# Moving the activation rows of the output projection and the feed-forward part by 80 bytes

## The chip, the cores and the metric

The kernel runs on one core of a Trainium2 chip. The metric is the device time of one execution in microseconds (us). TensorE (PE in the profile) multiplies, and its weight loads have a row of their own (PEld). VectorE (DVE) and ScalarE (ACT) do elementwise work, GpSimd (POOL) clears memory, SyncE (SP) issues the transfers. On-chip memory (SBUF) has 128 partitions; an address below is the byte offset within a partition, the same in all 128.

## The reference

One layer of a hybrid decoder works on 304 rows: 16 meta tokens, 256 prompt rows, and 8 samples of 4 rows. The parts that matter here are the dense projections; between the first two of them stand two token mixers (a recurrent one and a retention), which are left out.

```python
xn = f(rms_norm(x, norm_mix))
z = xn @ f(w_in)                                    # 2048 -> 7456
...
h = x + (jnp.concatenate([o_a, o_b], axis=-1) @ f(w_out)).astype(x.dtype)   # 2048 -> 2048
hn = rms_norm(h, norm_ffn)
h = h + (jax.nn.silu(hn @ w_gate) * (hn @ w_up)) @ w_down                   # 2048 -> 5632 -> 2048
```

The meta rows are dropped at the end, so the output projection and the feed-forward part need 288 rows only.

## The kernel before

**Layout.** Activations lie transposed: features in the partitions, tokens along the row. A matmul holds a block of 128 x 128 weights still and streams a row of 288 to 304 token columns past it into PSUM.

**Precision.** Weights and activations are split into two float32r parts, high and low. Each step of a product is three matmuls (lines 719 to 721): high weights by the high activations, high weights by the low ones, low weights by the high ones.

**Weights.** All projection weights come as one stream in the order of use (`sequence`, `steps`), 512 columns at a time: one transfer into `wr`, a cast on ACT into `wh` (`cast`), a subtraction on DVE into `wl` (`rest`), each in a ring of five buffers. `main` walks the steps, issues the three matmuls, and hands a finished accumulator to the job's `post`.

**Activations.** `xh` and `xl` hold 16 rows of XW = 320 columns each (1280 bytes). Three stages use them in turn. The input projection fills them in `convert` and streams columns c0 to 304 of every row; c0 is 0 for most tiles, 14 for the tiles called r of the recurrent mixer and for two small ones, and META = 16 for the tiles of the retention's q (line 1453, g = 0) and of its gate (line 1614), which so have 288 columns. The output projection's `prep` (lines 1711 to 1713) writes the mixers' results into columns 0 to 288, eight rows for each half. Then `hn` (line 748) writes the scaled residual into the same columns for the gate and up matmuls of the feed-forward part. The down matmuls stream `act` tiles, which `gu_post` (line 1736) makes: a high and a low row of 320 columns each, of which columns 0 to 288 are used. They come from a float32r arena with places that are planned ahead. `self.xs` is the list of row views that jobs are given.

**Order.** The feed-forward part goes through 5632 hidden features in 11 groups of four tiles of 128: the gate and up tiles of a group (16 steps each), then 16 down tiles (four steps each), with the first gate and up tiles of the next group put ahead of them. A planner (`Plan`) runs the whole program once with estimated times, writes down the order of work and the tiles' lifetimes, and the second run repeats that order. Its estimates go by shape and kind of an instruction, not by a column's position.

**Addresses.** In the built program, `xh` starts at 16512, `xl` at 36992 and the float32r arena at 215168. All are 128 past a multiple of 256, and 1280 is a multiple of 256, so each row of `xh`, `xl` and `act` starts 128 past a multiple of 256. The buffers of `wh` and `wl` start at 76608 and 86848 and follow each other by 2048; a block of 128 weight columns is 512 bytes, so every block that a matmul loads starts 64 past a multiple of 256.

Of the kernel before, what the change touches and what calls it, by code (L numbers as in the profile page):

```python
# [9 lines left out]
F32R = mybir.dt.float32r  # L10
I32 = mybir.dt.int32
AF = mybir.ActivationFunctionType
ALU = mybir.AluOpType
AX = mybir.AxisListType

P = 128
D = 2048
KT = D // P
# [4 lines left out]
T = META + SEQ + NB * NS  # L23
XW = T + 16
TO = SEQ + NB * NS
# [9 lines left out]
FSTEP = 4  # L35
# [33 lines left out]
for _n, _w in [("id", 128), ("blk", 128), ("mar", 256), ("lvl", 2 * 64), ("m16", 64), ("i16", 16), ("h16", 32), ("h32", 128), ("rst", TP),  # L69
               ("bm128", 8), ("ks", 12), ("kss", 4), ("qs", 128), ("own", 256), ("sel", 32)]:  # L70
    CV[_n] = _o
    _o += _w
NCV = _o


LASTK = T - P
# [67 lines left out]
def constants():  # L144

    f = np.float32
    c = np.zeros((P, NCV), f)
    put = lambda n, a: c.__setitem__((slice(0, a.shape[0]), slice(CV[n], CV[n] + a.shape[1])), a)
# [435 lines left out]
class Step:  # L584
# [163 lines left out]
    def hn(self, m):  # L748

        hm, gm = self.ht[m // 4][:, m % 4, :], self.pv("gffn", m)  # L750
        self.act.activation(self.xh[:, m, :TO], hm, AF.Copy, scale=gm)
        self.dve.scalar_tensor_tensor(self.xl[:, m, :TO], hm, gm, self.xh[:, m, :TO], op0=ALU.mult, op1=ALU.subtract)

    def rsqrt(self, src, scale, eps, floor=None, out=None):

# [81 lines left out]
    def constants(self):  # L837
# [5 lines left out]
        self.sp.dma_start(self.shin, I["shift"])  # L843
        self.cst = self.t([P, NCV], "cst", pool=self.cp)
        self.sp.dma_start(self.cst, I["cst"])
# [825 lines left out]
    def out_jobs(self, half):  # L1671

        dve, act = self.dve, self.act

        def post(m):
            def f(acc):
                if half == 0 and m % 4 == 0 and m < 12:
                    residual(m + 4)
                if half and m == 0:
                    self.ssq2 = self.t([P, TO], "ssq2")  # L1680
                hm = self.ht[m // 4][:, m % 4, :]
                dve.tensor_add(hm, hm, acc[:, :TO])
                if not half:
                    return
                yield
                if m < 8:
                    self.hn(m)
                if m == KT - 1:
                    for i in range(8, KT):
                        self.hn(i)  # L1690
                    self.done.add("hs")
                yield from self.sumsq(self.ssq2, hm, m == 0)
                if m == KT - 1:
                    yield
                    rstd = yield from self.rstd_from(self.ssq2)
                    self.rstd2 = self.t([P, TO], "rstd")
                    act.copy(self.rstd2, rstd)
                    self.done.add("rstd2")
            return f

        ks = range(8 * half, 8 * half + 8)

        def residual(m):
            ht = self.t([P, 4, TO], "ht")
            self.sp.dma_start(ht, xT(self.I)[:, m:m + 4, META:])
            self.ht.append(ht)

        def prep():
            if half == 0:
                residual(0)  # L1710
            for k in ks:
                act.copy(self.xh[:, k, :TO], self.os[k])
                dve.tensor_sub(self.xl[:, k, :TO], self.os[k], self.xh[:, k, :TO])

        need = lambda: all(("o", k) in self.done for k in ks)
        return [Job(("out", half, m), self.xs[8 * half:], post(m), cols=(0, TO),
                    need=None if m else need, prep=None if m else prep) for m in range(KT)]

    def ffn_jobs(self):
        dve, act = self.dve, self.act  # L1720
        hold = {}

        def gu_post(f, f0, up, acts, last):
            def g(acc):
                t = self.t([P, TO], "fu" if up else "fg")
                dve.tensor_mul(t, acc[:, :TO], self.rstd2)
                yield
                if not up:
                    act.activation(t, t, AF.Silu)
                    hold[f] = t  # L1730
                    return
                while f not in hold:
                    yield
                dve.tensor_mul(t, t, hold.pop(f))
                yield
                hl = self.t([P, 2, XW], "act", F32R)[:, :, :TO]
                act.copy(hl[:, 0, :], t)
                yield
                dve.tensor_sub(hl[:, 1, :], t, hl[:, 0, :])
                acts[f - f0] = hl[:, 0, :], hl[:, 1, :]  # L1740
                if last:
                    self.done.add(("act", f))
            return g

        def down_post(m, fin):
            def g(acc):
                hm = self.ht[m // 4][:, m % 4, :]
                if fin and m == KT - 1:

                    sq = self.t([P, TO], "sq2")  # L1750
                    third = [slice(c * TO // 3, (c + 1) * TO // 3) for c in range(3)]
                    for c in third:
                        dve.tensor_add(hm[:, c], hm[:, c], acc[:, c])
                    for c in third:
                        act.activation(sq[:, c], hm[:, c], AF.Square)
                    self.bridge()
                    yield
                    yield from self.final(sq)
                    return
                dve.tensor_add(hm, hm, acc[:, :TO])  # L1760
                if fin:
                    if m == 0:
                        self.ssq3 = self.t([P, TO], "ssq3")

                        root = self.t([P, 1], "root")
                        act.activation(root, self.ones[:, :1], AF.Sqrt)
                    yield
                    yield from self.sumsq(self.ssq3, hm, m == 0)
                    yield
                    act.activation(hm, hm, AF.Copy, scale=self.pv("gfin", m))  # L1770
            return g

        jobs = []
        for f0 in range(0, FT, FSTEP):
            f1 = min(f0 + FSTEP, FT)
            acts = {}
            for f in range(f0, f1):
                for up, name in enumerate(("gate", "up")):
                    jobs.append(Job((name, f), self.xs, gu_post(f, f0, up, acts, f == f1 - 1), cols=(0, TO),
                                    need=lambda: "hs" in self.done, ready="rstd2"))  # L1780
            for m in range(KT):
                jobs.append(Job(("down", f0, m), acts, down_post(m, f1 == FT), cols=(0, TO),
                                need=lambda f=f1 - 1: ("act", f) in self.done))
        return jobs
# [10 lines left out]
    def build(self, gam4):  # L1795
        self.gam4 = gam4
        self.shifts = 0
        self.os, self.on, self.gates, self.ht, self.xs_of = [None] * KT, {}, {}, [], {}
        self.xh = self.t([P, KT, XW], "xh", F32R, pool=self.cp)[:, :, :T]
        self.xl = self.t([P, KT, XW], "xl", F32R, pool=self.cp)[:, :, :T]  # L1800
        self.xs = [(self.xh[:, k, :], self.xl[:, k, :]) for k in range(KT)]
        jobs = [self.z_job(i, self.lora_post(i), c0=META - 2 if i else 0) for i in range(3)]
        for h in range(NPAIR):
            jobs += self.pair_jobs(h)
        for h in range(RH):
            jobs += self.ret_jobs(h) + self.gate_jobs(h)
        jobs += self.out_jobs(0) + self.out_jobs(1) + self.ffn_jobs()
        jobs = {j.key: j for j in jobs}
        self.raws, self.halves, self.rests, self.loaded, self.halved = [], [], [], 0, 0
        self.start()  # L1810
        self.plan.run(self.main(jobs))
        self.flush(all=True)
# [5 lines left out]
def xT(I):  # L1818

    return I["xT"][:, KT:].rearrange("p (k t) -> p k t", t=T)  # L1820
# [52 lines left out]
```

## Time and profile before

| | us |
|---|---|
| median of 3 runs | 1545.74 |
| lowest and highest | 1544.01, 1547.75 |
| span of the profiled execution | 1544.2 |
| PE busy | 1527.5 |
| weight loads busy | 1499.9 |
| DVE busy | 1089.4 |
| ACT busy | 866.5 |

The span is the time from the first to the last instruction of the one execution that was profiled; the device time of a run has some start and end around it. The input projection and the mixers fill the span up to some 594 us, the output projection goes on to some 695 us, the feed-forward part to 1533 us, and the last norm and the transfers out end it. A matmul's record lasts from its start to the end of its pipeline, about 294 ns here, while the next one starts some 130 ns later. The pace of TensorE is thus the distance between starts, and not the length of a record.

### The profile page before, as it was taken

How to read it: one execution, taken by the hardware profiler on the slowest of the kernel's cores; microseconds unless marked ns; L12 is line 12 of the kernel's file. 1: busy time of each engine (PE TensorE's matmuls, PEld its weight loads, DVE VectorE, ACT ScalarE, POOL GpSimd, SP SyncE). 2: the span in 40 equal slices, each digit the busy share in tenths (PEclk: the TensorE clock that was granted, in tenths of full speed). 3: DMA queues.
4: the chain of work that ended last, by engine and by line, in shares of the span. 5: the costliest groups of instructions: out<-in, count | busy, mean ns of one | idle time of the engine just before them, and what ended most of it. 6: DMA issues, size and time to landing. Idle time of an engine off the chain costs nothing.

```text
span 1544.2 us, 31919 instructions
## 1 busy us (share of the span) xinstructions
PE 1527.5 (99%) x11446; PEld 1499.9 (97%) x11446; DVE 1089.4 (71%) x2782; ACT 866.5 (56%) x2031; POOL 27.7 (2%) x161
## 2 busy tenths in 40 slices
PE   9999999999999999999999999999999999999997
PEld 8999999999999998999999999999999999999997
DVE  6989789899989878676656555556565656565656
ACT  6775876787876865555444444444444444444446
POOL 1000000000000000000000000000000000000000
PEclk9999999999999999999999999999999999999998
DMA  7544445434444576655555555555555555555553
GB/s 229 175 144 141 124 113 153 126 115 155 157 124 136 182 247 210 207 171 162 167 171 164 164 168 166 169 167 169 170 162 171 164 167 168 170 165 172 162 173 117
DMA packets 136334, 252.33 MB, mean 163 GB/s; under 512 B 15984, under 2 KB 22256, under 8 KB 136176
## 3 DMA queue, kind: packets, MB, share of 16 engines
q1 hardware_dynamic: 136176, 250.29, 53.5%
q8 instruction: 91, 1.49, 0.4%
q14 instruction: 67, 0.55, 0.1%
HBM read 235.95 MB, written 14.28 MB: 162 GB/s over the span
## 4 chain that ended last, share of the span: by engine, by line
PE 88%; DVE 7%; ACT 3%; issue 1%; DMA 0%; SPq 0%; DVEq 0%; ACTq 0%
PE acc L310 78%; PE mm L310 10%; DVE arena_dt.float L310 5%; ACT arena_dt.float L310 2%; DVE wl L310 2%; ACT wh L310 1%; DMA arena_dt.float<-xT 0%; SPq L310 0%; DVE arena_dt.float32r L310 0%; ACT arena_dt.float32r L310 0%; DVE xl L310 0%; ACT xh L310 0%; DVEq L1869 0%; ACT shout L310 0%; DVEq L310 0%
## 5 line engine op out<-in xcount | busy, mean ns | idle before, releaser
L310 PE MATMUL acc<-xh,wh 128*128 128x288 f32 (+2 forms) x2592 | 789.8, 305 | 2.6 <-ACT wh L310 1.8
L310 PE MATMUL acc<-xh,wl 128*128 128x288 f32 (+2 forms) x2592 | 765.5, 295 | 0.3 <-DVE wl L310 0.3
L310 PE MATMUL acc<-xl,wh 128*128 128x288 f32 (+2 forms) x2592 | 765.1, 295 | 0.1
L310 ACT CAST wh<-wr 128x512 fp32r<-128x512 f32 (+1 forms) x827 | 501.4, 616 | 350.8 <-PE acc L310 313.0
L310 DVE TENSOR_TENSOR wl<-wr,wh 128x512 fp32r<-128x512 f32 (+1 forms) x827 | 560.2, 685 | 131.0 <-ACT wh L310 128.1
L310 PEld LDWEIGHTS acc<-xh,wh 128*128 128x128 f32 x2592 | 486.2, 188 | 9.6 <-issue 3.7
L310 PEld LDWEIGHTS acc<-xl,wh 128*128 128x128 f32 x2592 | 486.0, 188 | 4.6 <-issue 1.2
L310 PEld LDWEIGHTS acc<-xh,wl 128*128 128x128 f32 x2592 | 485.3, 187 | 1.1 <-DVE wl L310 0.6
L310 PE MATMUL acc<-arena_dt.float32r,wh 128*128 128x288 f32 x1408 | 278.9, 294 | 0.4 <-ACT arena_dt.float32r L310 0.3
L310 PEld LDWEIGHTS acc<-arena_dt.float32r,wh 128*128 128x128 f32 x1408 | 224.9, 188 | 0.9 <-ACT arena_dt.float32r L310 0.6
L310 PE MATMUL acc<-arena_dt.float32r,wl 128*128 128x288 f32 x704 | 206.7, 294 | 0.0
L310 DVE TENSOR_TENSOR arena_dt.float<-acc,arena_dt.float 128x288 f32<-128x288 f32 (+4 forms) x181 | 72.7, 420 | 167.9 <-PE acc L310 167.6
L310 DVE TENSOR_TENSOR arena_dt.float<-arena_dt.float 128x288 f32<-128x288 f32 (+22 forms) x694 | 175.2, 286 | 12.0 <-ACT arena_dt.float L310 7.6
L310 ACT ACTIVATE arena_dt.float<-arena_dt.float 128x288 f32<-128x288 f32 (+7 forms) x245 | 104.6, 433 | 116.7 <-DVE arena_dt.float L310 114.8
L310 PE MATMUL mm<-arena_dt.float 128*128 128x128 f32 (+7 forms) x1136 | 167.7, 302 | 0.6 <-issue 0.2
L310 DVE TENSOR_TENSOR arena_dt.float<-arena_dt.float,acc 128x288 f32<-128x288 f32 (+1 forms) x210 | 94.4, 451 | 95.8 <-PE acc L310 95.6
L310 PEld LDWEIGHTS mm<-arena_dt.float 128*128 128x128 f32 (+1 forms) x1136 | 141.3, 181 | 11.4 <-issue 3.6
L310 PEld LDWEIGHTS acc<-arena_dt.float32r,wl 128*128 128x128 f32 x704 | 132.1, 188 | 0.0
L310 ACT COPY arena_dt.float<-mm 64x64 f32<-64x64 f32 (+11 forms) x330 | 91.4, 286 | 49.0 <-PE mm L310 44.0
L310 ACT CAST arena_dt.float32r<-arena_dt.float 128x288 fp32r<-128x288 f32 (+4 forms) x73 | 30.5, 422 | 91.1 <-DVE arena_dt.float L310 90.4
L310 ACT COPY arena_dt.float<-arena_dt.float 128x32 f32<-128x32 f32 (+7 forms) x235 | 57.1, 293 | 13.3 <-DVE arena_dt.float L310 11.5
L310 DVE SCALAR_TENSOR_TENSOR arena_dt.float<-arena_dt.float 128x288 f32<-128x288 f32 (+3 forms) x96 | 43.1, 451 | 2.3 <-ACT arena_dt.float L310 0.5
(66 smaller groups left out, 564.8 us busy)
## 6 DMA issues: line engine op xcount, KB each, us to landing
wr<-big SPq DMA_DIRECT2D x823, 256.0 KB, 2.8
arena_dt.float<-s0r SPq DMA_DIRECT2D x16, 512.0 KB, 5.2
out_rts<-arena_dt.float SPq DMA_DIRECT2D x16, 512.0 KB, 4.4
arena_dt.float<-xT SPq DMA_DIRECT2D x4, 576.0 KB, 4.7
arena_dt.float<-lora SPq DMA_DIRECT2D x16, 128.0 KB, 2.6
arena_dt.float<-s0w SPq DMA_DIRECT2D x8, 256.0 KB, 2.9
out_rws<-arena_dt.float SPq DMA_DIRECT2D x8, 256.0 KB, 3.5
out_y<-arena_dt.float SPq DMA_DIRECT2D x7, 288.0 KB, 2.4
```

Source lines behind the costliest of these rows:

```text
L310: return self._plan.keep(f(*a, **k))
```

## The change

Two lists give, for each of the 16 rows of `xh` and `xl` and for each of the 11 groups of `act` tiles, the column at which the 288 columns begin. All entries are 20 columns, 80 bytes, and 20 + 288 still fits into the 320. `self.xf` is the list of shifted row views. `prep`, `hn`, the output jobs and the gate and up jobs use it in place of the views that began at column 0; the act tiles are cut the same way. The input projection keeps its views and columns, and neither tile sizes nor weights are touched.

```diff
+SHIFT_X = [20] * KT
+SHIFT_A = [20] * 11
...
     def hn(self, m):
 
         hm, gm = self.ht[m // 4][:, m % 4, :], self.pv("gffn", m)
-        self.act.activation(self.xh[:, m, :TO], hm, AF.Copy, scale=gm)
-        self.dve.scalar_tensor_tensor(self.xl[:, m, :TO], hm, gm, self.xh[:, m, :TO], op0=ALU.mult, op1=ALU.subtract)
+        xh, xl = self.xf[m]
+        self.act.activation(xh, hm, AF.Copy, scale=gm)
+        self.dve.scalar_tensor_tensor(xl, hm, gm, xh, op0=ALU.mult, op1=ALU.subtract)
...
             for k in ks:
-                act.copy(self.xh[:, k, :TO], self.os[k])
-                dve.tensor_sub(self.xl[:, k, :TO], self.os[k], self.xh[:, k, :TO])
+                xh, xl = self.xf[k]
+                act.copy(xh, self.os[k])
+                dve.tensor_sub(xl, self.os[k], xh)
...
-        return [Job(("out", half, m), self.xs[8 * half:], post(m), cols=(0, TO),
+        return [Job(("out", half, m), self.xf[8 * half:], post(m), cols=(0, TO),
...
-                hl = self.t([P, 2, XW], "act", F32R)[:, :, :TO]
+                s = SHIFT_A[f0 // FSTEP]
+                hl = self.t([P, 2, XW], "act", F32R)[:, :, s:s + TO]
...
-                    jobs.append(Job((name, f), self.xs, gu_post(f, f0, up, acts, f == f1 - 1), cols=(0, TO),
+                    jobs.append(Job((name, f), self.xf, gu_post(f, f0, up, acts, f == f1 - 1), cols=(0, TO),
...
-        self.xh = self.t([P, KT, XW], "xh", F32R, pool=self.cp)[:, :, :T]
-        self.xl = self.t([P, KT, XW], "xl", F32R, pool=self.cp)[:, :, :T]
+        xh = self.t([P, KT, XW], "xh", F32R, pool=self.cp)
+        xl = self.t([P, KT, XW], "xl", F32R, pool=self.cp)
+        self.xh, self.xl = xh[:, :, :T], xl[:, :, :T]
+        self.xf = [(xh[:, k, s:s + TO], xl[:, k, s:s + TO]) for k, s in enumerate(SHIFT_X)]
         self.xs = [(self.xh[:, k, :], self.xl[:, k, :]) for k in range(KT)]
```

## The prediction, made before the changed kernel was run

> **What bounds the kernel now.** I read the page first: its busy times, then the chain that ended last.
>
> ```profile
> span 1544.2 us, 31919 instructions
> ## 1 busy us (share of the span) xinstructions
> PE 1527.5 (99%) x11446; PEld 1499.9 (97%) x11446; DVE 1089.4 (71%) x2782; ACT 866.5 (56%) x2031; POOL 27.7 (2%) x161
> ...
> PE 88%; DVE 7%; ACT 3%; issue 1%; DMA 0%; SPq 0%; DVEq 0%; ACTq 0%
> ```
>
> TensorE (PE) is the bound, but a busy share of 99% does not tell how fast it goes. That is read from the chain in order of time, from 590 us on (start, length, what, count), and from the busy times of one steady stretch.
>
> ```profile
> 611.50 90.06 PE acc L310 x684
> ...
> 705.91 799.13 PE acc L310 x6069
> ...
> 800.00:1400.00 600.00, 600.00 (x4559) 600.00 (x4558) 353.94 (x634) 253.82 (x443) 0.00 (x0) 1.00 0.56 167
> ```
>
> From 611 to 1505 us nothing but PE stands on the chain, and its pace is 799.13 us / 6069 = 131.67 ns per matmul (90.06 / 684 gives the same). In the steady stretch the granted clock is 1.00, DVE is busy 59%, ACT 42%, the DMA engines 56%: each waits for PE. So the output projection and the feed-forward part cost the number of their matmuls times the interval between two starts, and nothing else in that stretch can move the end.
>
> **What the change touches.** Moved are the rows that the matmuls of these two parts stream. Their number comes from the groups by shape (count | busy us, mean ns; a mean is the length of one matmul in a pipeline, not the interval).
>
> ```profile
> L310 PE MATMUL acc<-xh,wh 128*128 128x288 f32 x1920 | 572.1, 298 | 0.8 <-ACT xh L310 0.8
> L310 PE MATMUL acc<-xl,wh 128*128 128x288 f32 x1920 | 563.9, 294 | 0.1
> L310 PE MATMUL acc<-xh,wl 128*128 128x288 f32 x1920 | 563.6, 294 | 0.0
> L310 PE MATMUL acc<-arena_dt.float32r,wh 128*128 128x288 f32 x1408 | 278.9, 294 | 0.4 <-ACT arena_dt.float32r L310 0.3
> L310 PE MATMUL acc<-arena_dt.float32r,wl 128*128 128x288 f32 x704 | 206.7, 294 | 0.0
> ```
>
> Of each 1920, 256 belong to 16 tiles of the input projection that also have 288 columns (line 1453 with g = 0, line 1614), and they stay. So 3 x 1664 + 1408 + 704 = 7104 matmuls change their start address. **One ns of interval is worth 7.1 us, or 0.46%.** No instruction, DMA or wait is added or removed.
>
> **Does the start address matter?** The kernel holds its own comparison. Those 16 tiles have the same shape and precision, and weights that lie the same, but stream from column 16 on, 64 bytes later. In the built program the rows of xh, xl and act begin on multiples of 128 bytes and every block of weights 64 bytes past one. I call the lead the distance by which the moving row's start is ahead of the weight block's, modulo 128: it is 64 now, 0 in those tiles, 120 in the tiles of 290 columns that start at column 14 (56 bytes), and 16 after the change (80 - 64). The chain has a run of the first kind and one of the 304-column tiles (lead 64); the matmuls in order of time give the 290-column tiles (first and last of 48).
>
> ```profile
> 227.26 5.60 PE acc L310 x42
> ...
> 127.58 7.03 PE acc L310 x51
> ```
>
> ```profile
> 96.30 0.30 PE L310 MATMUL acc<-xh,wh 128*128 128x290 f32 x1
> ...
> 102.57 0.30 PE L310 MATMUL acc<-xh,wl 128*128 128x290 f32 x1
> ```
>
> Lead 0: 5.60 / 42 = 133.3 ns, 1.65 ns more than 131.67 at lead 64 for the same 288 columns. Lead 120: 6.27 / 47 = 133.4 ns; from 131.67 and from the 304 columns' 7.03 / 51 = 137.8, 290 columns at lead 64 would take 131.67 + 2 x 6.13 / 16 = 132.4. So leads 0 and 120 are dearer than 64 by 1.0 to 1.65 ns. Lead 16 is in no row.
>
> The Trainium skill says otherwise (SBUF — State Buffer, Who interferes with whom): TensorE has one read port for the moving operand and another for weight loads, and waits on no one. By that rule the sum is zero. The 133.3 against 131.67 does not agree with it, unless something else in the input stage slows those tiles.
>
> **What could cost the 1.65 ns, and what lead 16 does to it.** The weight load of the next matmul runs beside the current one. The load's length gives its speed, and 32-column tiles show what a short load leaves (start of the kernel, two clocks: the windows' last three columns are granted clock, DMA share, GB/s).
>
> ```profile
> L310 PEld LDWEIGHTS acc<-arena_dt.float32r,wh 128*128 128x128 f32 x1408 | 224.9, 188 | 0.9 <-ACT arena_dt.float32r L310 0.6 <-DVE arena_dt.float32r L310 0.3
> ...
> L310 PEld LDWEIGHTS mm<-arena_dt.float 128*32 128x32 f32 x128 | 3.3, 109 | 2.7 <-issue 1.3
> ```
>
> ```profile
> 13.14 0.44 PE L310 MATMUL acc<-xh,wh 128*32 128x290 f32 x1
> ...
> 15.07 0.44 PE L310 MATMUL acc<-xh,wl 128*32 128x290 f32 x1
> ...
> 18.89 0.29 PE L310 MATMUL acc<-xh,wh 128*32 128x290 f32 x1
> ...
> 20.06 0.30 PE L310 MATMUL acc<-xh,wh 128*32 128x290 f32 x1
> ```
>
> ```profile
> 12.90:15.10 2.20, 2.20 (x10) 1.57 (x11) 2.20 (x5) 2.20 (x6) 0.00 (x0) 0.50 1.04 405
> 18.80:20.20 1.40, 1.40 (x13) 1.15 (x13) 1.40 (x4) 1.40 (x3) 0.00 (x0) 1.00 0.83 210
> ```
>
> 96 more columns take 188 - 109 = 79 ns, so 128 take 105 ns, at 4.9 bytes per ns. The moving row goes 1152 / 131.67 = 8.75 bytes per ns. While a load lasts, the moving reader gains (8.75 - 4.9) x 105 = some 400 bytes on it. If the two disturb each other each time the gain passes a multiple of 128 bytes, the places are: lead 0 at 0, 128, 256, 384 (four); lead 120 at 8, 136, 264, 392 (four); lead 64 at 64, 192, 320, and 448 just beyond the reach; lead 16 at 112, 240, 368, and 496 far beyond. This is my account, not something a row states; it fits the order of the three leads. At lead 64 the fourth lies near the edge, and two rows show that the pace there is not one fixed number: in the last group, with the same leads, it differs (first and last matmul shown, 45 intervals apart).
>
> ```profile
> 1518.08 0.43 PE L310 MATMUL acc<-arena_dt.float32r,wh 128*128 128x288 f32 x2
> ...
> 1524.03 0.43 PE L310 MATMUL acc<-arena_dt.float32r,wh 128*128 128x288 f32 x2
> ```
>
> 5.95 us / 45 = 132.2 ns against 131.67. So I take it that lead 64 meets the fourth disturbance in some matmuls and not in others, and lead 16 never.
>
> The price of "never" is not in the trace. **Bounds:** from below, the 32-column tiles at full clock, 1.17 us / 9 = 130.0 ns for 290 columns, 129.1 for 288, which is what a load a quarter as long leaves: a gain of 2.55 ns, 18 us. (At half clock they take 1.93 us / 8 = 241 ns, so 120 at full speed; no row at full clock comes near it, and I do not reach for it.) From above, lead 0, the nearest row in bytes: 1.65 ns, 11.7 us lost. I take an even mixture of three and four at lead 64, so three alone is as far below 131.67 as four is above: 130.0 ns. The sum is 7104 x -1.65 ns = **-11.7 us**; the span goes from 1544.2 to 1532.5, and the median of the runs, 1.5 us above the span, from 1545.74 to **1534.0**.
>
> The Trainium skill's interval for one matmul (TensorE: Matmul & The Clock Gate, Back-to-back issue gap) is N / 2.4 + 2.5 ns; an estimate from that page is 122.5 ns for 288 columns, and the sum by it would be 65 us saved at most. No row here at full clock shows it.
>
> **What else the shift moves.** The rows are also written 80 bytes later: 32 rows of xh and of xl (8 of them before this answer's window, which starts at 590 us), and 44 act tiles.
>
> ```profile
> L310 ACT ACTIVATE xh<-arena_dt.float,pv x16: 519/536/538, 648.0 to 696.1; 128x288 fp32r<-128x288 f32 x16
> L310 DVE SCALAR_TENSOR_TENSOR xl<-arena_dt.float,pv,xh x16: 512/516/520, 648.5 to 698.3; 128x288 fp32r<-128x288 f32 x16
> L310 ACT CAST xh<-arena_dt.float x8: 427/430/431, 641.6 to 643.9; 128x288 fp32r<-128x288 f32 x8
> L310 DVE TENSOR_TENSOR xl<-arena_dt.float,xh x8: 449/450/452, 642.7 to 645.3; 128x288 fp32r<-128x288 f32 x8
> ```
>
> I cost this at nothing: if every write took half as long again, each engine would lose 32 x 0.25 = 8 us, most of it between 640 and 700 us, and 44 x 0.22 = 10 us over the feed-forward part, under 100% in both (59% and 42% busy above). Uncovered are only the last writes before the first gate tile and before the last group of down tiles, under 2 us in all. The planner books by shape, not by column, so the order of instructions stays. If PE gets faster by 1.3%, its feeders have room: 59% becomes 60%.
>
> **The rivals.**
> Slower: the disturbance repeats every 256 bytes, not 128. Then the leads are 64 (now), 128 and 120 (dear), and 144 after the change, beyond the dear ones. With a reach of 400 bytes, lead 64 passes at 192 and sometimes 448, leads 128 and 144 at 128, 384 and at 112, 368: two each. Lead 16 then takes 133.3 ns: +11.7 us, 1557.4. It decides from the point where the second passing falls inside the reach. For it speaks that the nearest row, 16 bytes away, is dear, and that 120 to 128 rises; against it, nothing but the fit of the other account.
> Same: lead 64 meets exactly three disturbances, as lead 16 does, and the 132.2 ns is an accident of the last group; or the input stage, not the address, makes its tiles slow. The short load (one passing at 8 bytes of gain, 129.1 ns) speaks for it: one at 129.1 and four at 133.3 make 1.4 ns each, so three come to 131.9, about what lead 64 has. Then 1545.7; the skill's rule of separate ports ends here too.
> That the change does not do what it says: only if readers and writers were shifted by different amounts, and both go through the same list of views (xf), so I give it nothing.
>
> **How the numbers follow.** This kernel's measurement tells about 0.2% (3 us) from no change, 0.44 ns per matmul. Faster, 1527 to 1542: 0.44. Same: 0.20. Slower, 1549 to 1560: 0.36. The range for all is 1526 to 1560: its low end is the 129.1 ns bound with 1.5 us for the spread of the runs, its high end the lead-0 price with 2 us for late writes.
>
> **What would show it.** In the changed profile the long piece of the chain from about 705 us should again have some 6069 matmuls, at 130.0 ns each (789 us instead of 799); 133.3 (809 us) proves the slower rival, 131.7 the same. The input stage's 133.3 and 137.8 ns must stay, and the output projection's run from 611 us must change by the same ns as the feed-forward part, since all three kinds of rows get the same lead. I am wrong altogether if the interval falls below 129 or rises above 134 ns, or if PE shows gaps there.

## The result, and the profile after

| | before | changed |
|---|---|---|
| median of 4 runs on the same chip, us | 1545.9 | 1535.11 |
| lowest and highest, us | 1544.01, 1547.75 | 1533.65, 1535.58 |
| span of the profiled execution, us | 1544.2 | 1533.1 |

The ratio of the times is 0.9932, with a 95% interval from 0.9918 to 0.9946: 10.8 us faster. The forecast was 1534.0.

The page of the changed kernel, its busy times and the shares of its chain by engine:

```profile
span 1533.1 us, 31919 instructions
...
PE 1516.7 (99%) x11446; PEld 1489.5 (97%) x11446; DVE 1089.1 (71%) x2782; ACT 866.7 (57%) x2031; POOL 27.7 (2%) x161
...
PE 93%; DVE 4%; ACT 1%; issue 1%; DMA 0%; SPq 0%; DVEq 0%; ACTq 0%
```

The counts of every engine are those of before, DVE's and ACT's busy times as well, to 0.3 us (1089.1 against 1089.4, 866.7 against 866.5): the writes that begin 80 bytes later cost nothing that can be seen. TensorE is less busy, its matmuls by 10.8 us and its weight loads by 10.4. The shares of the chain also changed, from 88% PE and 7% DVE before, but not by a gain: in the input projection, where the two kernels do not differ, PE and DVE are nearly tied, and the chain goes over one or the other (from 278 to 360 us over DVE and ACT before, over PE now). Where PE lost its time stands in the chain in order of time (start us, length us, what, count):

```profile
127.48 7.03 PE acc L314 x51
...
227.14 5.60 PE acc L314 x42
...
611.13 89.69 PE acc L314 x684
...
705.12 789.01 PE acc L314 x6069
...
1496.12 23.99 PE acc L314 x182
```

The first two rows are the input projection, whose rows were not moved: 7.03 and 5.60 us, as before. The long piece has the same 6069 matmuls as before and takes 789.01 us where it took 799.13: 130.0 ns each instead of 131.67, 10.1 us less. The output projection gives 90.06 - 89.69 = 0.4 us and now takes 131.1 ns per matmul; the last group of down tiles, which took 24.31 us before, gives 0.3 us. The piece of the output projection starts 0.4 us earlier. Together that is 11.2 us, the 11.1 us of the span within rounding.

### The profile page after: what moved, and what is told of

Same layout as the page of the kernel before. It is cut to its first block, busy times and chain, and to the rows that moved or that the text cites. A ratio compares the mean times of both kernels' runs of the same rounds, so it can differ in the third digit from the quotient of the medians.

```text
span 1533.1 us, 31919 instructions
## 1 busy us (share of the span) xinstructions
PE 1516.7 (99%) x11446; PEld 1489.5 (97%) x11446; DVE 1089.1 (71%) x2782; ACT 866.7 (57%) x2031; POOL 27.7 (2%) x161
## 4 chain that ended last, share of the span: by engine, by line
PE 93%; DVE 4%; ACT 1%; issue 1%; DMA 0%; SPq 0%; DVEq 0%; ACTq 0%
PE acc L314 82%; PE mm L314 12%; DVE arena_dt.float L314 3%; DVE wl L314 1%; DMA arena_dt.float<-xT 0%; SPq L314 0%; ACT arena_dt.float L314 0%; DVE arena_dt.float32r L314 0%; ACT wh L314 0%; ACT arena_dt.float32r L314 0%; ACT xh L314 0%; DVEq L1878 0%; DVE xl L314 0%; ACT shout L314 0%; DVEq L314 0%
## 5 line engine op out<-in xcount | busy, mean ns | idle before, releaser
L314 DVE TENSOR_TENSOR wl<-wr,wh 128x512 fp32r<-128x512 f32 (+1 forms) x827 | 559.6, 685 | 128.8 <-ACT wh L314 125.9
L314 PE MATMUL acc<-arena_dt.float32r,wh 128*128 128x288 f32 x1408 | 275.4, 293 | 0.4 <-ACT arena_dt.float32r L314 0.3
L314 PEld LDWEIGHTS acc<-arena_dt.float32r,wl 128*128 128x128 f32 x704 | 132.1, 188 | 0.0
```

The lines of the kernel that those rows point to most:

```text
L314: return self._plan.keep(f(*a, **k))
```

## The experiments

All diffs are against the changed kernel. "Start" is the column at which a moving row begins. "Lead" is the prediction's term, but here without the cut to 128 bytes: a row that starts at column c has its start 64 + 4c bytes ahead of a weight block's, counted modulo 256; it is also called the distance below. So the kernel before has lead 64, the changed one 144, the input projection's 288-column tiles have 128.

### Ten starts in one kernel, and the same in another order

Each of the 11 groups of act tiles gets its own start, so that the down tiles of one kernel show one start after another, while the gate and up tiles keep column 20:

```diff
-SHIFT_A = [20] * 11
+SHIFT_A = [0, 4, 8, 12, 16, 20, 24, 28, 32, 18, 20]
```

> The rows of xh and xl stay at 20 columns, and each of the eleven groups of act tiles gets its own start: 0, 4, 8, 12, 16, 20, 24, 28, 32, 18, 20 columns, so leads of 64, 80, 96, 112, 0, 16, 32, 48, 64, 8, 16 bytes. Read is the interval of the 192 down matmuls of each group. Theory (two readers disturb each other each time the moving one has gained a multiple of 128 bytes over the weights): lead 64 at 131.7 ns in both its groups, rising over 80 and 96 to 133.3 at 112 and 0, then a fall to 130.0 at 16 and 32, and 48 between 130.0 and 131.7. Rival (a repeat of 256 bytes): the two groups with lead 64, which are 128 bytes apart, differ by more than 1 ns. Rival (only the moving row's own start counts, odd multiples of 16 bytes are good): 4, 12, 20 and 28 columns all at 130.0, the multiples of 32 bytes at 131.7 to 133.3. Rival (the interval is a rhythm that a stream falls into, whatever the address): no order, and most groups stay at the 130.0 of the gate matmuls before them.

The windows of the first ten groups' down matmuls (act tiles alone; columns: window, its length, PE busy and count, granted clock, DMA share, GB/s):

```profile
758.16:783.80 25.64, 25.44 (x192) 1.00 0.57 163
833.36:858.90 25.54, 25.34 (x192) 1.00 0.58 164
908.88:934.53 25.65, 25.45 (x192) 1.00 0.57 161
984.51:1010.73 26.22, 26.01 (x192) 1.00 0.55 159
1060.28:1086.25 25.97, 25.76 (x192) 1.00 0.56 156
1135.80:1161.12 25.32, 25.12 (x192) 1.00 0.58 163
1210.68:1236.64 25.96, 25.76 (x192) 1.00 0.58 159
1286.20:1311.81 25.61, 25.40 (x192) 1.00 0.58 163
1361.36:1387.33 25.97, 25.76 (x192) 1.00 0.55 160
1436.88:1463.35 26.47, 26.26 (x192) 1.00 0.55 158
```

A window has 192 starts, so 191 intervals and one record of 0.30 us at the end: the first row gives (25.44 - 0.30) / 191 = 131.6 ns. The clock is full in all and the DMA share lies between 0.55 and 0.58, so of what the windows show nothing but the start column goes with the differences.

To see whether the place of a group in time, or the gate and up matmuls ahead of it, make the number, the groups were put in another order and the gate and up rows back to column 0:

```diff
-SHIFT_X = [20] * KT
-SHIFT_A = [20] * 11
+SHIFT_X = [0] * KT
+SHIFT_A = [20, 32, 28, 24, 20, 16, 12, 8, 4, 18, 20]
```

> The sweep of starts of the act tiles in another order (20, 32, 28, 24, 20, 16, 12, 8, 4, 18, 20 columns), with xh and xl at column 0, so that other matmuls run before each group. Theory (the lead modulo 256 decides): each start has the interval of the first sweep, 20: 130.0, 32: 133.3, 28: 131.5, 24: 133.3, 16: 133.3, 12: 134.6, 8: 131.7, 4: 131.1, 18: 136.0; the gate and up matmuls 131.7. Rival (history decides: the intervals are rhythms that a stream falls into): several starts off their first value by 1 ns or more.

Four windows of the same kind from this kernel (starts 20, 24, 12 and 18):

```profile
757.61:782.94 25.33, 25.13 (x192) 1.00 0.56 165
...
985.30:1011.25 25.95, 25.75 (x192) 1.00 0.57 160
...
1213.35:1239.56 26.21, 26.01 (x192) 1.00 0.56 157
...
1441.76:1468.22 26.46, 26.26 (x192) 1.00 0.56 155
```

Intervals worked out in this way from both kernels, in ns:

| start column | lead, bytes | first kernel | other order |
|---|---|---|---|
| 0 | 64 | 131.6 | not among its groups |
| 4 | 80 | 131.1 | 131.1 |
| 8 | 96 | 131.7 | 131.6 |
| 12 | 112 | 134.6 | 134.6 |
| 16 | 128 | 133.3 | 133.3 |
| 18 | 136 | 135.9 | 135.9 |
| 20 | 144 | 129.9 | 130.0 and 130.0 |
| 24 | 160 | 133.3 | 133.2 |
| 28 | 176 | 131.4 | 131.4 |
| 32 | 192 | 133.3 | 133.3 |

For these down matmuls the start decides; the place in time and the matmuls ahead don't, to 0.1 ns. (The gate and up matmuls between them did not all keep one pace; the section on breaks comes back to that.) Three things follow. The pattern does not repeat every 128 bytes: columns 0 and 32 are 128 bytes apart and differ by 1.7 ns. It is not smooth either: column 20 is the lowest of the ten, and its neighbours 18 and 24 are among the dear ones. And the counting account of the prediction cannot make it, since it gives the same three disturbances, 130.0 ns, to columns 20, 24 and 28, and to no tile more than four, 133.3 ns.

By the Trainium skill's rule that the prediction weighed (SBUF — State Buffer, Who interferes with whom), all rows of the table would be alike; with 129.9 against 135.9 ns in one kernel the measurement decides against it for these matmuls.

### Only the weights moved: is it the distance, or the row's own address?

The weights lie 128 bytes later, the moving rows where the changed kernel has them (a small tile ahead of the weights grows, and a pad ahead of the float32r arena shrinks by as much; other buffers between the two move along, but no matmul compared here reads them):

```diff
-GAP = 56
+GAP = 24
...
-        self.omu = self.t([P, 46], "omu", pool=self.cp)
+        self.omu = self.t([P, 78], "omu", pool=self.cp)
```

> The changed kernel with all weight buffers 128 bytes later. Theory (the pattern repeats every 128 bytes): nothing changes, 130.0 ns in the feed-forward part, 133.3 and 137.8 ns in the input projection. Rival (it repeats every 256 bytes): the lead modulo 256 goes from 144 to 16, and the feed-forward part's interval moves by 1 ns or more.

The chain of this kernel in order of time, its run of 288-column input tiles, output projection and long piece:

```profile
226.86 5.53 PE acc L314 x42
...
611.12 88.92 PE acc L314 x684
...
704.38 799.12 PE acc L314 x6069
```

The moving rows begin where they did, and the long piece is back at 799.12 / 6069 = 131.67 ns; the output projection went the other way, 88.92 / 684 = 130.0, and the input tiles, whose rows nobody moved, from 133.3 to 5.53 / 42 = 131.7. So the row's own address does not decide alone; where the weights lie counts too. A move of the weights by 128 bytes changes the paces, so from this side too there is no repeat of 128 bytes. One distance, 16 bytes, has two paces in this kernel, 130.0 ns in the output projection and 131.67 in the long piece.

### Both moved: is it the distance alone?

Weights and rows both 64 bytes earlier, then both 32 bytes earlier, so that the distance is the changed kernel's:

```diff
-SHIFT_X = [20] * KT
-SHIFT_A = [20] * 11
-GAP = 56
+SHIFT_X = [4] * KT
+SHIFT_A = [4] * 11
+GAP = 72
...
-        self.omu = self.t([P, 46], "omu", pool=self.cp)
+        self.omu = self.t([P, 30], "omu", pool=self.cp)
```

> All weight buffers begin 64 bytes earlier and the activation rows 16 bytes late in place of 80: the lead is 16 as in the changed kernel, with other addresses on both sides. In the input projection the leads become 0 for the 304-column tiles and 64 for the 288-column tiles. Theory (the lead decides): 130.0 ns in the feed-forward part, 131.7 ns in the input projection's 288-column tiles instead of 133.3, and the 304-column tiles above 137.8 by 1 to 2 ns. Rival (the moving row's own start decides, 80 bytes past a multiple of 128 is good): the feed-forward part away from 130.0, the input projection as it was (133.3 and 137.8).

This run, at 1655.47 us, is inconclusive for its question: TensorE was granted 0.85 of its clock throughout. One window of its steady stretch (columns: window, length, busy time of PE, PEld, DVE, ACT and POOL, clock, DMA share, GB/s), and from its chain the run of 288-column input tiles and the long piece:

```profile
800.00:1400.00 600.00, 600.00 (x4255) 600.00 (x4254) 332.75 (x596) 237.24 (x414) 0.00 (x0) 0.85 0.53 156
```

```profile
242.41 5.93 PE acc L314 x42
...
756.23 856.45 PE acc L314 x6069
```

The long piece, at distance 144, takes 856.45 / 6069 = 141.1 ns, and the input tiles, at distance 192, 5.93 / 42 = 141.2. In the sweep at full clock these two distances lay 3.3 ns apart; the last section comes back to it. The 32-byte pair ran at full clock:

```diff
-SHIFT_X = [20] * KT
-SHIFT_A = [20] * 11
-GAP = 56
+SHIFT_X = [12] * KT
+SHIFT_A = [12] * 11
+GAP = 64
...
-        self.omu = self.t([P, 46], "omu", pool=self.cp)
+        self.omu = self.t([P, 38], "omu", pool=self.cp)
```

> Second attempt at moving both sides: weights 32 bytes earlier (32 past a multiple of 256) and activation rows 48 bytes late, so the lead is again 16 modulo 128 and 144 modulo 256, as in the changed kernel, with other addresses on both sides. Theory (the distance between the two rows decides): 130.0 ns in the feed-forward part. Rival (the moving row's own start, or the weights' own, decides): another interval, by 1 ns or more.

Its chain:

```profile
612.09 89.69 PE acc L314 x684
...
706.09 795.75 PE acc L314 x6069
```

This one run took 1542.68 us. The output projection takes what it takes in the changed kernel, 131.1 ns. The long piece takes 131.1 too, where the changed kernel has 130.0. At the same distance two paces occur, and the changed kernel has both: 131.1 in its output projection, 130.0 in its feed-forward part. Next is whether it is the address that picks one, or what ran before.

### Two paces of one distance: breaks in the stream

One small filler step is put into the middle of the second half of the output projection and into each group of down tiles; addresses and work stay:

```diff
+            if k == 0 and (key == ("out", 1, 8) or key[0] == "down" and key[2] == 8):
+                self.bridge(1)
```

> The changed kernel with one more small matmul (a 128-column float32 product that nothing reads) put into the stream at 12 places: in the middle of the second half of the output projection and in the middle of the down tiles of each group. Theory (lead and history: the changed kernel ran the output projection at 131.1 and the feed-forward part at 130.0 ns with the same lead, so a break can move the stream from the one rhythm to the other): the output projection after its break, or some groups after theirs, change between 130.0 and 131.1. Rival (the output projection is slower for a cause of its own, its accumulators or the engines beside it): no interval changes, 131.1 before and after the break in the output projection, 130.0 everywhere in the feed-forward part.

Its chain, from the output projection past the second break (this part of the view ends at 790 us) and around a later one:

```profile
609.88 57.82 PE acc L314 x441
667.71 0.22 PE mm L314 x2
667.93 31.61 PE acc L314 x243
...
703.83 65.71 PE acc L314 x501
769.54 0.22 PE mm L314 x2
769.77 20.29 PE acc L314 x156
...
919.98 75.52 PE acc L314 x576
995.50 0.22 PE mm L314 x2
995.72 74.89 PE acc L314 x576
```

57.82 / 441 = 131.1 ns ahead of the break, 31.61 / 243 = 130.1 behind it, in the same tiles with the same addresses. In the feed-forward part 65.71 / 501 = 131.2 goes over to 20.29 / 156 = 130.1, and of the later pieces between two breaks some take 75.52 / 576 = 131.1 and some 74.89 / 576 = 130.0. So at one pair of addresses what came before picks the pace, and in these traces it holds until something breaks the stream. Not every break switches it: of the first ten in the feed-forward part seven do.

The kernels without breaks show the same where tiles of different starts follow each other. In the sweep the gate and up matmuls, all at distance 144, run at 131.1 ns in some groups (47.07 us for 359 from 860 us on) and at 130.0 in others (47.19 us for 363 from 1012 us on). In the kernel of the other order they are at distance 64, and two stretches of its chain are:

```profile
861.97 46.08 PE acc L314 x350
```

```profile
936.98 47.07 PE acc L314 x356
```

These are 131.7 and 132.2 ns: distance 64 has two paces as well, and the 132.2 that the prediction found in the last group of the kernel before is the second one.

The same breaks with both addresses 64 bytes earlier (the first diff of the section before, and this one), now at full clock:

> Weights 64 bytes earlier and activation rows 16 bytes late (the lead of the changed kernel once more, third pair of addresses, as in the run that met a lower clock), with the 12 breaks of the bridge run. Theory (the lead fixes which rhythms there are, history which of them runs): only 130.0 and 131.1 ns, both of them, in the output projection and the feed-forward part, and the input projection's 288-column tiles, now at lead 192, off 133.3 only if lead 192 has another rhythm than lead 128 (the sweeps gave 133.3 for it as well). Rival (the run with weights 32 bytes earlier stood at 131.1 throughout because its addresses make it so): a single interval, or intervals other than these two.

```profile
611.09 57.33 PE acc L314 x441
668.42 0.22 PE mm L314 x2
668.64 31.59 PE acc L314 x243
...
704.54 65.71 PE acc L314 x501
770.25 0.22 PE mm L314 x2
770.47 74.88 PE acc L314 x576
```

In this chain too only the two paces occur: 130.0 (57.33 / 441, 74.88 / 576) and 131.2 (65.71 / 501); only the first of the ten breaks switches them here. Its 288-column input tiles, at distance 192, take what the sweep gave for it:

```profile
226.87 5.60 PE acc L314 x42
```

That is 133.3 ns, as expected. At three pairs of addresses with distance 144 the long stages took 130.0 or 131.1 ns and no third value at full clock: **at this distance the paces are these two, at all three pairs of addresses, and the history picks one of them.** Both kernels with breaks, at 1538.63 and 1537.04 us in one run each, gain nothing on the changed one.

### Short weight blocks: does the load make the difference?

The ten starts again, while the down matmuls load only 32 of the 128 columns of a weight block:

```diff
-SHIFT_A = [20] * 11
+SHIFT_A = [0, 4, 8, 12, 16, 20, 24, 28, 32, 18, 20]
...
-            self.pe.matmul(acc[:m, :n], hi[:, o:o + m], xh, start=k == 0, stop=False)
-            self.pe.matmul(acc[:m, :n], hi[:, o:o + m], xl, start=False, stop=False)
-            self.pe.matmul(acc[:m, :n], lo[:, o:o + m], xh, start=False, stop=k == K - 1)
+            c = 32 if key[0] == "down" else m
+            self.pe.matmul(acc[:c, :n], hi[:, o:o + c], xh, start=k == 0, stop=False)
+            self.pe.matmul(acc[:c, :n], hi[:, o:o + c], xl, start=False, stop=False)
+            self.pe.matmul(acc[:c, :n], lo[:, o:o + c], xh, start=False, stop=k == K - 1)
```

> As the sweep of eleven starts, but the down matmuls load and compute only the first 32 of their 128 weight columns (the other 96 rows of the feed-forward part's result are left out). A load then lasts a quarter as long, some 26 ns, in which the moving reader gains some 100 bytes. Theory (the weight load is what disturbs the moving stream): the groups lie closer together than in the sweep with full loads, at 129 to 130 ns, at most one disturbance apart (1.1 to 1.7 ns). Rival (the moving row alone sets the interval by its start): the same differences between the groups as in the sweep with full loads, up to 3 ns.

Five of its windows (starts 4, 8, 12, 20 and 18), the columns as in the first experiment:

```profile
831.56:857.52 25.96, 25.75 (x192) 1.00 0.58 160
907.08:932.19 25.11, 24.91 (x192) 1.00 0.61 167
982.17:1007.50 25.33, 25.14 (x192) 1.00 0.57 165
...
1132.07:1157.40 25.33, 25.12 (x192) 1.00 0.57 163
...
1432.48:1458.03 25.55, 25.34 (x192) 1.00 0.56 162
```

The dear starts lose their price: column 12 falls from 134.6 to (25.14 - 0.30) / 191 = 130.1 ns, column 18 from 135.9 to 131.1. Eight of ten starts lie between 129.9 and 131.1. Two don't: column 8 goes down to 128.8, and column 4 goes up, from 131.1 to 133.2 with a quarter of the load. So most of the difference between the starts hangs on the weight block: with a quarter of it the dear starts are no longer dear. The edit shortens the load that runs beside the matmul, but the same edit also has the matmul compute 32 result rows instead of 128, so that it is the load, and not the narrower product, is likely and not shown. A simple count of overlapping bytes does not explain the values, and column 4 stays unexplained.

### The input projection moved as well, and the changed kernel once more

The input projection's rows begin 4 columns later, which brings its 288-column tiles to the changed kernel's distance:

```diff
-        self.xh, self.xl = xh[:, :, :T], xl[:, :, :T]
+        self.xh, self.xl = xh[:, :, 4:4 + T], xl[:, :, 4:4 + T]
```

> The changed kernel with the input projection's rows begun 4 columns (16 bytes) late too. Its 288-column tiles then have the lead of the shifted parts (144 modulo 256), the 304-column tiles 80, the 290-column tiles 136. By the sweep: 288 columns 130.0 instead of 133.3, 304 columns at or up to 1 ns below 137.8, 290 columns 2 to 3 ns above 133.4 (18 columns, lead 136, was at 136.0). Sum where TensorE is the bound: 768 x -3.3, 1536 x -0.5 and 432 x +2.5 ns, about -2 us. Rival (the input stage's tiles are slow for another cause): 133.3 stays.

Over the matmuls that follow one another in the trace, the 288-column tiles went from 133.3 to some 130.5 ns, as the distance says. The 304-column tiles went from 137.8 to some 138.5, where no change or a small gain was expected. The 290-column tiles now have lead 136, the dearest of the table, and got faster, from 133.4 to 132.1: the table, made with 288 columns, does not carry over to other widths. The one run took 1533.52 us, and a comparison with the changed kernel on one chip followed:

> The kernel with the input projection's rows 16 bytes late as well, timed on the same chip as the changed kernel. Theory (its 288-column tiles gain 2.8 ns and its 290-column tiles 1.6 ns, its 304-column tiles lose 0.5 to 1 ns): 768 x -2.8, 432 x -1.6 and 1536 x +0.7 come to -1.8 us if TensorE is the bound there: a ratio 0.0012 below the changed kernel's. Rival (in that stage waits for the mixers absorb it): the same time as the changed kernel.

> The changed kernel unaltered, as the yardstick for the other and to see whether the rhythm it falls into is the same each time. Theory: ratio 0.9932 again, output projection at 131.1 and feed-forward part at 130.0 ns. Rival (the rhythm is a matter of chance from run to run): the feed-forward part at 131.1 in some runs, which would cost 7 us, so times some 7 us apart.

1533.24 us (1532.95 to 1535.18, ratio 0.9929, interval 0.9916 to 0.9941) against 1533.36 for the changed kernel (1533.02 to 1535.48, ratio 0.993, 0.9916 to 0.9944): no difference, though the 1.8 us that were forecast lie within the intervals. The profiles tell more. In the first run of the kernel with the moved input the output projection starts at 609.74 us, in the repeat of the changed kernel at 609.58. The chain of the first:

```profile
609.74 89.69 PE acc L314 x684
```

The same chain in the repeat of the changed kernel:

```profile
609.58 89.69 PE acc L314 x684
...
703.57 789.01 PE acc L314 x6069
```

Counted from the start of a run of 72 matmuls early on (26.76 and 26.63 us), the output projection begins 582.98 and 582.95 us later; in the second profile of the moved input, whose start took longer, it is 582.69 (611.56 after 28.87). The 768 matmuls at some 2.7 ns less are 2.1 us, and with what the other two widths lose and gain the sum is still more than 1 us. At the output projection 0.3 us of it at most are left. Where they can go is seen in the chain by line between 220 and 240 us, of the kernel with the moved input (its second profile):

```profile
by line: DVE arena_dt.float L314 38.8%; PE acc L314 30.5%; DVE wl L314 21.4%; issue 5.5%; PE mm L314 3.6%; DVEq L314 0.4%
```

and of the changed kernel in the same stretch:

```profile
by line: PE acc L314 90.3%; PE mm L314 10.9%
```

In this stretch the chain changed from PE to VectorE: a faster PE waits there. That the whole gain goes this way was not followed through the stage. The repeat has the same two paces in the same stages, to 0.01 us (89.69 and 789.01), and its five times lie within 2.5 us, not the 7 us apart that another pace would cost: between these runs the pace of a stage is not a matter of chance.

## Why the prediction was right, and where its reasons were wrong

- **The bound.** PE's interval times its matmuls, with nothing beside it in that stretch: right. Nearly the whole gain is in the rows of PE on the chain, and 6069 matmuls stand in the long piece before and after.
- **7104 matmuls, -1.65 ns, -11.7 us.** Right for the feed-forward part: 130.0 ns and 789 us were forecast, 789.01 measured. The output projection failed it: forecast to change by the same ns, it went from 131.67 to 131.1, 0.4 us instead of the 1.1 us that 684 x 1.65 ns make. The experiment with breaks shows why: one distance has two paces, and this stage entered the other one. That is most of why the span gained 11.1 us and not 11.7. The median lies 2.0 us above the profiled span, where the forecast added 1.5: 1535.11 instead of 1534.0.
- **The same reason could have cost most of the gain.** With both addresses 32 bytes earlier the long piece takes 795.75 us, 6.7 us more at the same distance. The forecast had no term for this.
- **"The Trainium skill says otherwise".** The prediction set the measured 133.3 against 131.67 above the rule of separate ports, with the reservation that the input stage might slow its tiles. The reservation is gone: down tiles at the input tiles' lead, column 16, take the same 133.3 ns.
- **What could cost the 1.65 ns.** The distance between row and weights decides, as the account said (weights moved alone change it), and weight blocks a quarter as wide take most of it away. The account itself, "a disturbance each time the gain passes a multiple of 128 bytes", is wrong: columns 24 and 28 were to be as cheap as 20 and are at 133.3 and 131.4, columns 12 and 18 are above all that it allows, and 0 and 32 columns differ. Nor does the "even mixture" of three and four at lead 64 stand behind the size: lead 64 has steady paces, 131.67 and 132.2 ns. That lead 16 came out at 130.0, in direction and in size, was luck: the sum was right from a wrong mechanism, and four columns further, with the same count, it would have been 133.3.
- **The bounds.** The dear end, 133.3 from the nearest row, held for the changed kernel but is not the worst that an address costs: column 18 takes 135.9, which as the start of all 7104 would be 7104 x 4.2 ns, some 30 us, above before, outside the range. "Wrong altogether above 134 ns" was drawn too close. The cheap end, 129.1, held for full loads; with short ones column 8 reached 128.8.
- **The slower rival** was right that nothing repeats after 128 bytes, and wrong in its conclusion: of the ten leads, 144 lies between two dear ones, 136 and 160, and is the cheapest. **The same rival**, three disturbances each, falls with the counting, and the 132.2 ns that it took for an accident of the last group is the second pace of lead 64; its other half, that the input stage slows its own tiles, falls with the 133.3 ns of the down tiles at lead 128. **That the change doesn't do what it says** falls with the interval itself.
- **Writes at nothing, order unchanged.** Right: DVE's and ACT's busy times and all counts are as before.

What stays open: what in the chip makes this pattern of distances and its paces, whether it repeats at 256 bytes or further, whether a distance has more paces than were met here, and why column 4 gets dearer with a short load. Of the versions run that compute the whole result none beats the changed kernel measurably.

## What to carry to other kernels

Where TensorE bounds a stage, its interval per matmul is worth a test of addresses: put one start per group into one kernel and read the interval group by group, since ten starts 8 to 16 bytes apart showed 4.6% between them and no rule was found that would have named the best. What such a sweep gives belongs to the distance between rows and weights, not to the start column, and to one tile width; whoever moves a buffer ahead of the weights changes that distance too. And a stage at one distance can hold either of two paces, so look at each stage's own interval before a gain is put down to an address.

## What the hardware showed that was not expected

- The start of a row moves the interval of a 288-column matmul between 129.9 and 135.9 ns at full clock, with weights, work, granted clock and DMA load the same.
- The same addresses run at one of two steady paces, 130.0 or 131.1 ns, for hundreds of matmuls; a break of 0.22 us can switch between them, and in a repeat of the kernel each stage took the pace that it had before. Distance 64 has two paces as well (131.67 and 132.2 ns), and so has distance 16 (130.0 and 131.67).
- At a granted clock of 0.85 two distances that differ at full clock did not: 141.1 ns at distance 144 and 141.2 at distance 192, where the kernel with breaks, at the same addresses and full clock, took 130.0 to 131.1 and 133.3. If the interval goes with the clock, 141.1 ns is 119.9 ns at full speed; the 290-column tiles at half clock, 241 ns in the prediction, give 120.5, at another distance. At full clock no run came below 128.8 for 288 columns. So some 10 ns of the 130.0 and 13 of the 133.3 show only at full clock. The dearest distances were not met at the lower clock.
- The Trainium skill (TensorE: Matmul & The Clock Gate, Back-to-back issue gap) gives an isolated matmul the stream alone at the cold clock and 2.5 ns on top at the warm one. In kind the trace agrees, since an extra cost shows only at full clock; in size not: in this stream, with a weight load for each matmul, the rows with full loads lie 7 to 13 ns above the 122.5 ns that the prediction estimated from it.
